# Lower parts of the first branch's, the gates' and the output projection's weights made by GpSimd, their products queued last

## The chip, the cores and the metric

The kernel runs on one core of a Trainium2 chip. The metric is the time of one execution on the device in microseconds (us), the median of several executions. An engine works through its own queue in order and waits at an instruction until the semaphores that it names have been raised: TensorE multiplies (PE in the profile, its weight loads PEld), VectorE (DVE) and ScalarE (ACT) do elementwise work, GpSimd (POOL) can do elementwise work too and cannot read PSUM, the memory that TensorE writes its sums to. SyncE (SP) issues DMAs.

## The reference

One layer of a diffusion backbone, for 512 latent tokens and 256 context tokens of 1024 channels, in 32-bit floats:

```python
h = rms_norm(x, g_norm1) * (1.0 + sc1) + sh1
aq, ak, av, dq, dk, dv, dz, da, db, ga, gd = split_cols(h @ w_in)
...
y_attn = window_ctx_attention(q_a, k_a, v_a, k_ac, v_ac, attn_sink)
o_dl, _, _ = bidir_delta(*dn_inputs(dq, dk, dv, da, db), s_cf, s_cb)
...
y_d = (rms_norm(o_d, dn_norm_g) * jax.nn.silu(heads(z, DN_HEADS))).reshape(z.shape)
y = jax.nn.sigmoid(gate_a) * (y_a @ w_br_attn) + jax.nn.sigmoid(gate_d) * (y_d @ w_br_dn)
...
x_new = x.astype(jnp.float32) + gt1 * merge(y_attn, o_dl, dz, ga, gd)
x_new = x_new + gt2 * mlp(x_new, sh2, sc2)
```

`bidir_delta` is a recurrence over chunks of 64 tokens in both directions, first over the context and then over the latent tokens. The MLP has 4096 hidden channels.

## The kernel before

**Products in three passes.** TensorE multiplies in a reduced 32-bit format (fp32r). To keep the accuracy, each operand is split into an upper part, the value rounded to that format, and a lower part, the rest. A product is the sum of three: upper weight by upper activation, upper weight by lower activation, lower weight by upper activation. A tile of 128 output channels with 1024 inputs has 8 blocks k and so 24 matmuls of 128x128 by 128x512; one with 512 inputs (a branch projection) has 4 blocks and 12 matmuls.

**Weights.** `wload` fetches a tile through SyncE's queue into one of four staging slots (`wr`), has ScalarE write the upper part (line 259) and then makes the lower part in one of three ways: line 266 subtracts on VectorE (raw minus upper); for the 14 attention and recurrence tiles (`late`), ScalarE writes the negated upper part and a DMA from GpSimd's queue adds the raw weights to it (lines 263 and 264). Upper and lower parts of the list `wq` have two slots each, `wh` and `wl`; the MLP's weights have buffers of their own (`m`). `wnext` hands out a tile and starts the load of the one after it, so that one tile is loaded ahead.

**The list.** After the 14 `late` tiles come 44 with line 266: three gate tiles of the second branch (kind GD), 8 tiles of the first branch's projection (`wbr[0]`, 4 blocks each), 17 gate tiles (8 GA, 4 DZ, 5 GD, 8 blocks each), 8 tiles of the second branch's projection (`wbr[1]`, 4 blocks) and 8 of the output projection (`wout`, 8 blocks).

**Who consumes them.** `gate_tiles` (line 1028) and `br_a` (line 1073) are generators that yield after each matmul: the recurrence's code runs some of their matmuls between its own steps (`run_fill`, `run_both`), as cover for the recurrence's waits. A step of the recurrence (`chain_step`) has for each direction: TensorE's products with the state (line 1152), VectorE's lines 1156 and 1157, TensorE's line 1164, VectorE's line 1170, TensorE's lines 1185 and 1189, VectorE's line 1201, which makes the next state. VectorE also makes later modulation vectors (`late_mod`, line 1094), spread over the same time. The second branch and the output projection use `mm3` (lines 317 to 319), which runs the three passes block by block. The second branch's result goes through lines 1348 and 1350 (VectorE) and a split (line 184 on ScalarE, line 185 on VectorE) into `Y`, the output projection's input. The last three output tiles are multiplied in column halves of 256, with `mm3` too, so that the next norm can begin on the first half; they hold three weight tiles, where `wh` and `wl` have two slots each.

**Order.** The program is written in one order, and a planner in the framework puts each engine's instructions in the order in which it expects them to become ready, by its own durations; the queues are fixed when the kernel is built. GpSimd's queue has, beside the 14 DMAs, memsets of 32x512 between the recurrence's matrices (lines 900, 901, 1288, 1289).

Of the kernel before, what the change touches and what calls it, by code (L numbers as in the profile page):

```python
# [12 lines left out]
ALU = mybir.AluOpType  # L13
# [21 lines left out]
ND1 = 3  # L35
# [3 lines left out]
KT = D // P  # L39
# [60 lines left out]
def tile_layer(ctx: ExitStack, tc: tile.TileContext, I: dict, out: bass.AP, dbg=None):  # L100
    nc = tc.nc
    V, A, G, PE = nc.vector, nc.scalar, nc.gpsimd, nc.tensor
# [30 lines left out]
    r32 = lambda ap: ap.bitcast(F32R)  # L133
# [116 lines left out]
        nc.sync.dma_start(out=raw, in_=src)  # L250
        return raw

    def wload(src, n=KT, bufs=None, raw=None, late=False):
        raw = wfetch(src, n) if raw is None else raw
        if bufs:
            hi, lo = (b.ap.rearrange("p (k c) -> p k c", k=KT) for b in bufs)
        else:
            hi, lo = (sb.tile([P, KT, P], F32, tag=t, bufs=NWS, name=nm(t))[:, :n] for t in ("wh", "wl"))
        h = A.activation(r32(hi), raw, AF.Copy)  # L259
        if not early:  # L260
            tc.add_manual_dep(h.ins, row_[0].ins.name, nosync, reason="behind the first row")
        if late:
            A.activation(r32(lo), hi, AF.Copy, scale=-1.0)
            G.dma_start(out=r32(lo), in_=src, accum_op=ALU.add)
        else:
            V.tensor_tensor(r32(lo), raw, hi, op=ALU.subtract)  # L266
        return r32(hi), r32(lo)

    early, EARLY = [], {T_DK: 0, T_DK + 1: 0, T_DK + 2: 0, T_DK + 3: 1}
# [39 lines left out]
            hs.pop(0)[0].free()  # L309


    def mm3(acc, w, xs, start=True, stop=True, ks=None):
        ks = list(range(len(xs))) if ks is None else ks
        n = len(ks)
        for i, k in enumerate(ks):
            xhi, xlo = xs[i]
            PE.matmul(acc, w[0][:, k, :], xhi, start=(start and i == 0), stop=False)  # L317
            PE.matmul(acc, w[0][:, k, :], xlo, start=False, stop=False)  # L318
            PE.matmul(acc, w[1][:, k, :], xhi, start=False, stop=(stop and i == n - 1))  # L319

    def modulate(t, src, r, sc, sh, hi, lo, eng=V):
        V.scalar_tensor_tensor(t, src, sc, r, op0=ALU.mult, op1=ALU.mult)
# [5 lines left out]
    hx, hc = [], []  # L328
# [11 lines left out]
    for kt in range(KT):  # L340
        t = alloc(512)
# [31 lines left out]
    for b in [wab_, xs_, cs_, rstd, scb]:  # L373
# [3 lines left out]
    gates = [(T_GD, i) for i in range(ND1)] + [(T_GA, i) for i in range(8)] + [(T_DZ, i) for i in range(4)]  # L377
    gates += [(T_GD, i) for i in range(ND1, 8)]
    wq = [(I["win"][t], KT, None, None, True) for t in (T_AK, *range(T_AQ, T_AQ + 3), T_AV, T_AQ + 3, *range(T_DV, T_DV + 4),
                                                        *range(T_DQ, T_DQ + 4))]  # L380
    wq += [(I["win"][t + i], KT) for t, i in gates[:ND1]]
    wq += [(I["wbr"][0, ct], 4) for ct in range(8)] + [(I["win"][t + i], KT) for t, i in gates[ND1:]]
    wq += [(I["wbr"][1, ct], 4) for ct in range(8)] + [(I["wout"][ct], KT) for ct in range(8)]
    wq = [lambda a=a: wload(*a) for a in wq]
    wn = [wq.pop(0)()]

# [298 lines left out]
    t, t2 = alloc(TOK), alloc(TOK)  # L685
# [18 lines left out]
    for q, (w, acc) in enumerate(early):  # L704
        conv(kT[q][:, :SEQ], acc.ap, 4 + q)
        acc.free()
        acc = bank()
# [310 lines left out]
    gat = []  # L1018
    szt, gdt = [], []

    def gate_tiles(todo):

        for kind, i in todo:
            w = wnext()
            acc = bank()
            for k in range(KT):
                for p, (x, y) in enumerate(((0, 0), (0, 1), (1, 0))):
                    PE.matmul(acc.ap, w[x][:, k, :], hx[k][y], start=(k == p == 0), stop=(k == KT - 1 and p == 2))  # L1028
                    yield
            if kind == T_GA:  # L1030
                g = alloc(SEQ)
                act(g.ap, acc.ap, AF.Tanh, scale=0.5)
                V.scalar_tensor_tensor(gat[i].ap, g.ap, 1.0, gat[i].ap, op0=ALU.add, op1=ALU.mult)
                g.free()
            else:
                t = alloc(SEQ, True)
                if kind == T_GD:
                    act(t.ap, acc.ap, AF.Tanh, scale=0.5)
                else:
                    silu2(t.ap, acc.ap)  # L1040
                (gdt if kind == T_GD else szt).append(t)
            acc.free()
# [22 lines left out]
    def br_a():  # L1065

        for ct in range(8):
            gat.append(alloc(SEQ, True))
            w = wnext()
            pa = bank()  # L1070
            for j in range(4):
                for p, (x, y) in enumerate(((0, 0), (0, 1), (1, 0))):
                    PE.matmul(pa.ap, w[x][:, j, :], r32(Q[y][:, :, j, :]), start=(j == p == 0), stop=(j == 3 and p == 2))  # L1073
                    yield
            A.activation(gat[ct].ap, pa.ap, AF.Copy)
            pa.free()
        for b in Qb:
            b.free()
# [263 lines left out]
    for ct in range(8):  # L1342
        w = wnext()
        run_late(ct % 2)
        pd = bank()
        mm3(pd.ap, w, [(r32(b[:, :512]), r32(b[:, 512:])) for b in yd])
        g = gdt[ct].ap
        V.scalar_tensor_tensor(g, g, 1.0, pd.ap, op0=ALU.add, op1=ALU.mult)
        pd.free()
        V.tensor_tensor(g, g, gat[ct].ap, op=ALU.add)  # L1350
        split(g, Y[ct][:, :512], Y[ct][:, 512:])
# [25 lines left out]
    for ct in range(8 - NHALF):  # L1377
        w = wnext()
        acc = bank()
        mm3(acc.ap, w, ys)  # L1380
        run_late(2)
        residual(ct, acc, slice(0, 512))
        acc.free()
# [203 lines left out]
```

## Time and profile before

| | |
|---|---|
| median of 3 executions | 911.67 us (911.41 to 916.42) |
| the profiled execution | 911.22 us, its span 909.5 us |
| PE busy | 97% of the span |
| DVE busy | 64% |
| ACT busy | 50% |
| POOL busy | 25.2 us, 40 instructions |

The span runs from the first instruction's start to the last one's end; 911.22 - 909.5 = 1.7 us lie around it. The page of the profile shows how long each engine was busy. A matmul's row lasts until its modelled end, and the next one starts before that, so PE's rows overlap and its busy share does not tell how dense its work is: start times do. In a list of waits, "A <- B: total, times, longest" says that A's engine stood idle ahead of A until B had ended. A timeline row gives start and length in us, engine, line, operation and tiles, and the idle time before it in brackets. A window row gives the stretch, its length, the busy time of each engine and the count of its instructions, the clock, and the DMA share.

By time, the first 295 us hold the norms, the input projections, attention and the preparation of the recurrence; from 295 to 376 and a little on, the context steps and the matrices of the latent steps, with the first branch's projection and gate tiles in between; to 470 the latent steps with gate tiles; from about 486 to 509 the second branch's projection, to 554 the output projection, and then the MLP to the end.

### The profile page before, as it was taken

What the parts mean: (1) busy time and instruction counts of PE and PEld (TensorE: products, weight loads), DVE (VectorE), ACT (ScalarE), POOL (GpSimd) and SP (SyncE); (2) the same over time, 40 slices, a digit from 0 to 9 for tenths busy, and PEclk for the clock granted to TensorE, in tenths of its full rate; (3) what the DMA queues carried; (4) which work ended last, traced back from release to release, by engine and by line L of the source; (5) the groups of instructions that cost most, each with busy time, mean ns of one, the idle gap of its engine ahead of it and who ended that gap; (6) DMA issues with size and microseconds to landing.
All of it is one profiled execution on the core that took longest, in us unless ns stands there. A gap on an engine that the chain in (4) does not pass through costs nothing.

```text
span 909.5 us, 16844 instructions
## 1 busy us (share of the span) xinstructions
PE 879.4 (97%) x7082; PEld 704.7 (77%) x7082; DVE 585.4 (64%) x999; ACT 454.9 (50%) x819; POOL 25.2 (3%) x40
## 2 busy tenths in 40 slices
PE   8999999999899999999999999999999999999998
PEld 5668777867677787777678789888888888888886
DVE  3578799887778997677867988941654335324511
ACT  6588755476568786465663445630452134113400
POOL 0010001010000002010000000000000000000000
PEclk9999999999999999999999999999999999999999
DMA  8671455533001133633316773640553224322111
GB/s 355 262 230 21 92 117 120 112 71 58 13 13 35 56 110 94 207 98 95 117 37 219 245 245 135 227 144 1 188 157 95 70 73 150 103 69 79 38 47 46
DMA packets 30460, 105.59 MB, mean 116 GB/s; under 512 B 3760, under 2 KB 4400, under 8 KB 29360
## 3 DMA queue, kind: packets, MB, share of 16 engines
q1 hardware_dynamic: 28368, 97.18, 33.1%
q0 software_dynamic: 2016, 7.34, 5.0%
q8 instruction: 55, 0.90, 0.4%
q14 instruction: 21, 0.17, 0.1%
HBM read 102.41 MB, written 2.10 MB: 115 GB/s over the span
## 4 chain that ended last, share of the span: by engine, by line
PE 80%; DVE 10%; ACT 5%; issue 2%; DMA 1%; SPq 0%; DVEq 0%; ACTq 0%
PE banks L319 16%; PE banks L317 16%; PE banks L318 16%; PE banks L1028 9%; PE banks L424 5%; PE banks L1073 2%; PE banks L429 2%; PE banks L586 2%; PE banks L596 1%; PE banks L1164 1%; ACT m L148 1%; PE banks L662 1%; PE banks L1185 1%; PE banks L1152 1%; PE banks L210 1%
## 5 line engine op out<-in xcount | busy, mean ns | idle before, releaser
L317 PE MATMUL banks<-m,m 128*128 128x512 f32 (+1 forms) x600 | 223.6, 377 | 2.6 <-DVE m L643 1.6
L318 PE MATMUL banks<-m,m 128*128 128x512 f32 (+1 forms) x600 | 224.5, 376 | 0.1
L319 PE MATMUL banks<-m,m 128*128 128x512 f32 (+1 forms) x600 | 224.2, 376 | 0.0
L259 ACT ACTIVATE m<-wr 128x1024 fp32r<-128x1024 f32 x68 | 71.8, 1059 | 155.1 <-PE banks L318 74.0
L317 PEld LDWEIGHTS banks<-m,m 128*128 128x128 f32 x600 | 111.8, 188 | 26.0 <-ACT m L323 2.8
L318 PEld LDWEIGHTS banks<-m,m 128*128 128x128 f32 x600 | 112.5, 188 | 21.9 <-DVE m L324 1.5
L319 PEld LDWEIGHTS banks<-m,m 128*128 128x128 f32 x600 | 112.4, 188 | 21.3 <-issue 1.2
L266 DVE TENSOR_TENSOR m<-wr,m 128x1024 fp32r<-128x1024 f32 x68 | 82.8, 1224 | 62.8 <-ACT m L259 31.2
L1028 PE MATMUL banks<-m,wh 128*128 128x512 f32 x320 | 104.5, 405 | 1.5 <-issue 0.8
L1471 DVE SCALAR_TENSOR_TENSOR m<-banks,modT,m 128x512 f32<-128x512 f32 x32 | 24.0, 750 | 105.3 <-PE banks L319 105.3
L259 ACT ACTIVATE wh<-wr 128x1024 fp32r<-128x1024 f32 (+1 forms) x58 | 54.6, 941 | 50.6 <-issue 11.4
L424 PE MATMUL banks<-m,wh 128*128 128x512 f32 (+1 forms) x320 | 75.9, 374 | 1.2 <-DVE m L823 1.2
L1028 PEld LDWEIGHTS banks<-m,wh 128*128 128x128 f32 x320 | 58.0, 188 | 14.2 <-issue 1.0
L1028 PE MATMUL banks<-m,wl 128*128 128x512 f32 x160 | 64.7, 405 | 0.0
L424 PEld LDWEIGHTS banks<-m,wh 128*128 128x128 f32 x320 | 53.0, 189 | 11.5 <-issue 1.9
L266 DVE TENSOR_TENSOR wl<-wr,wh 128x1024 fp32r<-128x1024 f32 (+1 forms) x44 | 45.2, 1028 | 16.6 <-ACT wh L259 16.5
L184 ACT ACTIVATE m<-m 128x512 fp32r<-128x512 f32 (+1 forms) x56 | 34.8, 629 | 38.1 <-DVE m L1454 21.5
L185 DVE TENSOR_TENSOR m<-m,m 128x512 fp32r<-128x512 f32 (+1 forms) x56 | 38.3, 689 | 21.6 <-ACT m L184 21.3
L1094 DVE SCALAR_TENSOR_TENSOR m<-wa,m 128x1024 f32<-128x1024 f32 x32 | 39.0, 1223 | 12.6 <-DMA wa<-in_wada 7.4
L317 PE MATMUL banks<-m,wh 128*128 128x512 f32 (+1 forms) x120 | 42.0, 352 | 0.0
L319 PE MATMUL banks<-m,wl 128*128 128x512 f32 (+1 forms) x120 | 42.0, 351 | 0.0
L318 PE MATMUL banks<-m,wh 128*128 128x512 f32 (+1 forms) x120 | 41.8, 349 | 0.0
(241 smaller groups left out, 1371.8 us busy)
## 6 DMA issues: line engine op xcount, KB each, us to landing
wr<-in_wm SPq DMA_DIRECT2D x64, 512.0 KB, 3.7
wr<-in_win SPq DMA_DIRECT2D x38, 512.0 KB, 3.7
wa<-in_wada SPq DMA_DIRECT2D x32, 512.0 KB, 4.1
m<-in_wada SPq DMA_DIRECT2D x8, 1024.0 KB, 12.3
wl<-in_win POOLq DMA_DIRECT2D x14, 512.0 KB, 5.7
m<-in_xT SPq DMA_DIRECT2D x8, 512.0 KB, 5.6
wr<-in_wbr SPq DMA_DIRECT2D x16, 256.0 KB, 2.6
wr<-in_wout SPq DMA_DIRECT2D x8, 512.0 KB, 4.6
```

Of the source, the lines that this page charges most:

```text
L184: A.activation(r32(hi), src, AF.Copy)
L185: (eng or V).tensor_tensor(r32(lo), src, hi, op=ALU.subtract)
L259: h = A.activation(r32(hi), raw, AF.Copy)
L266: V.tensor_tensor(r32(lo), raw, hi, op=ALU.subtract)
L317: PE.matmul(acc, w[0][:, k, :], xhi, start=(start and i == 0), stop=False)
L318: PE.matmul(acc, w[0][:, k, :], xlo, start=False, stop=False)
L319: PE.matmul(acc, w[1][:, k, :], xhi, start=False, stop=(stop and i == n - 1))
L424: PE.matmul(a, w[0][:, k, :], x, start=(k == 0 and x is xs[k][0]), stop=False)
L429: PE.matmul(a, w[1][:, k, :], xs[k][0], start=False, stop=(k == KT - 1))
L1028: PE.matmul(acc.ap, w[x][:, k, :], hx[k][y], start=(k == p == 0), stop=(k == KT - 1 and p == 2))
L1094: V.scalar_tensor_tensor(t.ap, wa, 0.5, scr.ap, op0=ALU.mult, op1=ALU.mult, accum_out=modT[:, grp, j:j + 1])
L1471: V.scalar_tensor_tensor(xn_[ct], acc.ap, modT[:, 3, ct:ct + 1], xn_[ct], op0=ALU.mult, op1=ALU.add)
```

## The change

Three things are edited.

1. `wload` gets an argument `eng`, by default VectorE, and the 41 tiles of the list from the first branch's projection on (all but the `late` ones and the first three gate tiles) have their lower part subtracted by GpSimd.
2. The order of a tile's matmuls in `gate_tiles` and `br_a`: first all products with the upper part of the weights (two for each block), then those with the lower part. The count of matmuls is the same, and so is that of yields.
3. `mm3` gets an argument `after` that does the same, and it is set for the second branch's projection and the first five tiles of the output projection. The last three, in halves, keep the old order.

```diff
-    def wload(src, n=KT, bufs=None, raw=None, late=False):
+    def wload(src, n=KT, bufs=None, raw=None, late=False, eng=V):
...
-            V.tensor_tensor(r32(lo), raw, hi, op=ALU.subtract)
+            eng.tensor_tensor(r32(lo), raw, hi, op=ALU.subtract)
...
-    def mm3(acc, w, xs, start=True, stop=True, ks=None):
+    def mm3(acc, w, xs, start=True, stop=True, ks=None, after=False):
...
-            PE.matmul(acc, w[1][:, k, :], xhi, start=False, stop=(stop and i == n - 1))
+            if not after:
+                PE.matmul(acc, w[1][:, k, :], xhi, start=False, stop=(stop and i == n - 1))
+        for i, k in enumerate(ks if after else ()):
+            PE.matmul(acc, w[1][:, k, :], xs[i][0], start=False, stop=(stop and i == n - 1))
...
-    wq += [(I["wbr"][0, ct], 4) for ct in range(8)] + [(I["win"][t + i], KT) for t, i in gates[ND1:]]
-    wq += [(I["wbr"][1, ct], 4) for ct in range(8)] + [(I["wout"][ct], KT) for ct in range(8)]
+    wg = [(I["wbr"][0, ct], 4) for ct in range(8)] + [(I["win"][t + i], KT) for t, i in gates[ND1:]]
+    wg += [(I["wbr"][1, ct], 4) for ct in range(8)] + [(I["wout"][ct], KT) for ct in range(8)]
+    wq += [(*a, None, None, False, G) for a in wg]
...
+    def lo_last(n):
+        return [(0, y, k) for k in range(n) for y in range(2)] + [(1, 0, k) for k in range(n)]
...
-            for k in range(KT):
-                for p, (x, y) in enumerate(((0, 0), (0, 1), (1, 0))):
-                    PE.matmul(acc.ap, w[x][:, k, :], hx[k][y], start=(k == p == 0), stop=(k == KT - 1 and p == 2))
-                    yield
+            for p, (x, y, k) in enumerate(lo_last(KT)):
+                PE.matmul(acc.ap, w[x][:, k, :], hx[k][y], start=(p == 0), stop=(p == 3 * KT - 1))
+                yield
...
-        mm3(pd.ap, w, [(r32(b[:, :512]), r32(b[:, 512:])) for b in yd])
+        mm3(pd.ap, w, [(r32(b[:, :512]), r32(b[:, 512:])) for b in yd], after=True)
...
-        mm3(acc.ap, w, ys)
+        mm3(acc.ap, w, ys, after=True)
```

`br_a` is edited as `gate_tiles` is, with 4 blocks in place of 8.

More of the change, by code (lines that the diff above doesn't have):

```diff
@@ L1070, in br_a @@
             pa = bank()
[L1071 to L1074, printed above, removed]
+            for i, (x, y, j) in enumerate(lo_last(4)):
+                PE.matmul(pa.ap, w[x][:, j, :], r32(Q[y][:, :, j, :]), start=(i == 0), stop=(i == 11))
+                yield
             A.activation(gat[ct].ap, pa.ap, AF.Copy)
```

## The prediction

> **What bounds the kernel now.** I read the page's head first (which engine is full), then the busy time by stage, then the waits in the stages that the change touches, then single instructions at those waits.
>
> ```profile
> span 909.5 us, 16844 instructions
> ...
> PE 879.4 (97%) x7082; PEld 704.7 (77%) x7082; DVE 585.4 (64%) x999; ACT 454.9 (50%) x819; POOL 25.2 (3%) x40
> ...
> core 0: us, PE busy (x) PEld busy (x) DVE busy (x) ACT busy (x) POOL busy (x), PEclk, DMA share, GB/s
> 562.00:909.50 347.50, 343.43 (x1558) 285.56 (x1556) 149.97 (x184) 102.61 (x134) 0.00 (x0) 1.00 0.32 100
> 486.00:509.00 23.00, 23.00 (x100) 18.28 (x99) 20.86 (x35) 10.85 (x17) 0.00 (x0) 1.00 0.75 247
> 509.00:554.00 45.00, 44.98 (x262) 39.36 (x261) 36.84 (x57) 17.09 (x24) 0.00 (x0) 1.00 0.73 236
> 295.00:400.00 105.00, 102.86 (x1514) 79.94 (x1510) 83.71 (x147) 72.16 (x153) 9.21 (x16) 1.00 0.38 119
> 400.00:470.00 70.00, 65.71 (x1328) 50.82 (x1329) 50.89 (x118) 42.69 (x143) 0.00 (x0) 1.00 0.28 85
> ```
>
> The matrix engine PE is busy 879.4 of 909.5 us, at a granted clock of 1.00 in every row. From 562 us to the end the two MLP products run 1558 matmuls in 347.5 us with PE busy 343.43, and nothing that the change edits is in there. Before the first branch's first weights all instructions stay what they are. So the question is the stretch between. In 295 to 400 PE idles 105 - 102.86 = 2.1 us, in 400 to 470 4.3 us, from 486 to 554 nothing. These 6.4 us are about all that an engine off PE can hand back there: 0.7% of the run, less than the 1% that a measurement of this kernel can tell from no change. PE's own work in the stretch (the same matmuls and weight loads, in another order) stays.
>
> A row of PE is 0.39 us long where the next starts 0.23 us later, so the real pace has to come from start times:
>
> ```profile
> 504.76 0.40 PE L317 MATMUL banks<-m,wh 128*128 128x512 f32 x1
> ...
> 505.68 0.40 PE L318 MATMUL banks<-m,wh 128*128 128x512 f32 x1
> 505.98 0.50 PE L319 MATMUL banks<-m,wl 128*128 128x512 f32 x1
> 506.32 0.39 PE L317 MATMUL banks<-m,wh 128*128 128x512 f32 x1
> ```
>
> The five starts from 504.76 to 505.68 are 0.23 us apart (0.92 / 4). A tile of 12 matmuls (a branch projection) takes 2.8 us at that pace, one of 24 (a gate or output tile) 5.6 us. At 505.98 the lower-part matmul (line 319, operand wl) starts 0.07 us late, and the next 0.34 later: it waited for its weights.
>
> ```profile
> DVE wl L266 <- ACT wh L259: 16.5, 15, 3.5
> ...
> PEld banks L1164 <- DVE m L1157: 4.0, 6, 1.2
> ...
> PEld banks L319 <- DVE wl L266: 0.8, 4, 0.3
> ```
>
> Lateness of lower parts costs PE's weight loads 0.8 us in four places, all in the dense stage. The large wait is that of the chain step's product (line 1164) for VectorE's line 1157: 4.0 us in six places, as its weight loads show it. VectorE (DVE) itself stood 16.5 us behind ScalarE's upper parts. So the lower parts hurt mainly by standing in VectorE's queue ahead of the chain.
>
> **The change part by part.** *Moved off VectorE.*
>
> ```profile
> L266 DVE TENSOR_TENSOR wl<-wr,wh 128x1024 fp32r<-128x1024 f32 x28 | 34.2, 1223 | 16.2 <-ACT wh L259 16.1
> ...
> L266 DVE TENSOR_TENSOR wl<-wr,wh 128x512 fp32r<-128x512 f32 x16 | 11.0, 686 | 0.4 <-ACT wh L259 0.4
> ...
> L901 POOL MEMSET m<- 32x512 f32 x6 | 3.1, 522 | 134.2 <-PE banks L1185 125.8 <-PE banks L586 8.3
> ...
> L1288 POOL MEMSET m<- 32x512 f32 x4 | 3.0, 744 | 23.5 <-DVE m L1285 23.5
> ```
>
> Of the 28 subtracts of 128x1024 three (the first gate tiles) stay; 25 x 1.223 and 16 x 0.686 = 41.6 us leave VectorE. What PE gets of it is to be read where a chain waits:
>
> ```profile
> 394.34 1.23 DVE L266 TENSOR_TENSOR wl<-wr,wh 128x1024 fp32r<-128x1024 f32 x1 [2.44 <-ACT wh L259]
> 395.48 1.28 DVE L1278 TENSOR_TENSOR m<-m,banks 128x512 f32<-128x512 f32 x2
> ...
> 399.92 0.75 DVE L1157 SCALAR_TENSOR_TENSOR m<-m,m 128x256 f32<-128x256 f32 x2
> ...
> 393.32 1.10 PE L777 MATMUL banks<-m,m 64*32 64x64 f32 x64
> ...
> 400.48 1.15 PE L1164 MATMUL banks<-m,m 64*64 64x64 f32 x32 [1.74 <-DVE m L1157]
> ...
> 434.26 1.22 DVE L266 TENSOR_TENSOR wl<-wr,wh 128x1024 fp32r<-128x1024 f32 x1
> 435.39 0.42 DVE L1157 SCALAR_TENSOR_TENSOR m<-m,m 128x256 f32<-128x256 f32 x1
> ...
> 435.87 0.68 PE L1164 MATMUL banks<-m,m 64*64 64x64 f32 x16 [1.09 <-DVE m L1157]
> ```
>
> At 394.34 the subtract (1.23 us) stands ahead of line 1278 (395.48), whose product (line 777) ended at 393.32 + 1.10 = 394.42; VectorE is then busy without a gap to line 1157, for which PE waits 1.74 us at 400.48. Without it, line 1278 starts 1.0 us sooner: -1.0. At 434.26 the subtract stands directly ahead of line 1157 (435.39), and PE waits 1.09 us: -1.1. Of the 0.8 us of late lower parts, 0.6 goes (the rest is the last tile, below). Together -2.7 us. The 16.5 us of VectorE's own waiting goes too, but no other wait of PE in these rows ends on it, so I give it nothing more.
>
> *The price on GpSimd.* No row shows GpSimd (POOL) with two inputs. The nearest is its memset of 512 elements per partition, 0.52 us, so 1.0 us for 1024: the low end, with nothing read. Two inputs and one output, each at that pace, give 3.1 us, and 4.3 with one VectorE instruction of 1.22 us ahead of it: the high end. I take 2.1 us for 1024 and 1.05 for 512, the memset's pace twice, since the row is nearest in kind (one pass of the port each way). The 41 subtracts are then 69 us on an engine that was busy 25.2. [...]
>
> *Cover for the slower subtract.* The lower matmuls now come after 16 (or 8) upper ones: 16 x 0.23 = 3.7 us (or 1.8) more time, against 2.1 - 1.22 = 0.9 us (or 0.4) more work. Before, no gate or branch matmul waits for a lower part ahead of the dense stage. So 0, at the high price too (3.1 us more against 3.7). The weight staging buffer (four slots) is held 0.9 us longer and its next DMA issue on SyncE's queue waits as long; the upper part's slot comes free 8 matmuls, 1.9 us, sooner, so ScalarE waits less. PE waits for neither: 0. On GpSimd's queue the subtracts meet the memsets of lines 900, 901, 1288 and 1289; a memset behind a subtract comes up to 2.1 us late, which would show in the chain's next product, and a subtract behind a memset that waits has a tile of time and more. I take 0; the high end is one such delay, 2.1.
>
> *The last output tiles* are the place without cover: they run in column halves with the old order (the lower part third), and two slots serve three tiles.
>
> ```profile
> 546.20 1.22 DVE L266 TENSOR_TENSOR wl<-wr,wh 128x1024 fp32r<-128x1024 f32 x1
> ...
> 547.24 0.28 PE L318 MATMUL banks<-m,wh 128*128 128x256 f32 x1
> 547.48 0.38 PE L319 MATMUL banks<-m,wl 128*128 128x256 f32 x1
> ```
>
> The eighth tile's lower part ends at 547.42 and PE's lower matmul starts at 547.48, 0.24 after its predecessor where 0.12 is the pace of half tiles: just in time. On GpSimd it ends 0.9 us later: +0.9 (from 0, if other matmuls are queued between, to 3.1 at the high price).
>
> *The shared way into SBUF.* Where the two engines meet in this trace:
>
> ```profile
> 386.03 0.74 POOL L1288 MEMSET m<- 32x512 f32 x1 [12.86 <-DVE m L1285]
> ...
> 385.55 1.83 DVE L1285 COPY m<-m 32x512 f32<-32x512 f32 x4
> ```
>
> Four copies of line 1285 take 1.83 us on VectorE, and the memsets of line 1288 that lie among them take 744 ns on average, where those of line 901, of the same shape, take 522. The two engines hold each other up by some 0.2 us. If a subtract that reads on GpSimd holds up VectorE's two-input instructions for its whole length, line 1157 is one of them (m<-m,m in its row). In 400 to 470:
>
> ```profile
> L266 DVE TENSOR_TENSOR wl<-wr,wh 128x1024 fp32r<-128x1024 f32 x6 | 7.3, 1223 | 5.0 <-ACT wh L259 5.0
> L1157 DVE SCALAR_TENSOR_TENSOR m<-m,m 128x256 f32<-128x256 f32 x16 | 6.5, 421 | 0.2
> ```
>
> Six subtracts and eight pairs of line 1157 (0.81 us a pair): a pair meets a subtract with 6 x (2.1 + 0.8) / 70 = 0.25, so two pairs do, held 1.05 us on average; the queued gate matmuls cover about half: +1.0 (ends 0 and 6.6, below).
>
> *The order.* Instruction order on each queue comes from the framework's planner, with its own durations: the source has the gate tiles after all transposes, the trace has not.
>
> ```profile
> 473.34 0.48 PE L1028 MATMUL banks<-m,wh 128*128 128x512 f32 x1
> 473.66 1.06 PE L1323 MATMUL banks<-c_ident,m 128*128 128x128 f32 x8
> ```
>
> A GpSimd subtract in its plan shifts what is queued next to what, in the whole stretch. I take 0; the ends are the 3.7 us of PE's idle that are left after -2.7, either way.
>
> Sum: -2.7 + 0.9 + 1.0 = -0.8 us on the profiled execution's 911.22 gives 910.4. The median of the three runs is 911.67, 0.45 above that execution, which would make it 910.9. I put 910.6.
>
> **The rivals.** *The port binds the chain (916.0).* Every subtract in 400 to 470 holds up a pair for its full 2.1 us, of which the queued matmuls hide 1.0: 6 x 1.1 = 6.6 in place of 1.0, so 911.2 - 2.7 + 0.9 + 6.6 = 916.0. For it: the 744 against 522 ns. Against: VectorE's chain instructions mostly take one input from PSUM (lines 1156, 1170), and the subtract starts after ScalarE's upper part, at the tile's border, where few pairs stand. [...]
>
> *GpSimd cannot keep the pace of the second branch (slower, 924).* From 486 to 509 a tile lasts 2.8 us.
>
> ```profile
> L1350 DVE TENSOR_TENSOR m<-m,m 128x512 f32<-128x512 f32 x7 | 4.8, 685 | 0.0
> L1348 DVE SCALAR_TENSOR_TENSOR m<-m,banks 128x512 f32<-128x512 f32 x7 | 4.8, 682 | 0.9 <-PE banks L319 0.9
> L185 DVE TENSOR_TENSOR m<-m,m 128x512 fp32r<-128x512 f32 x6 | 4.1, 690 | 1.1 <-ACT m L184 1.0
> L1094 DVE SCALAR_TENSOR_TENSOR m<-wa,m 128x1024 f32<-128x1024 f32 x3 | 3.7, 1223 | 4.4 <-PE banks L1028 4.4
> ```
>
> Per tile VectorE has 0.69 + 0.69 us of two-input work and half an instruction of 1.22 (2.0 us), and the subtract comes on top if they exclude each other. Before, VectorE did 2.0 + 0.68 + 0.69 = 3.35 us per tile and ended 8 x 0.57 = 4.6 us late without idling PE. The loss is then 8 x (2.0 + x - 2.8) - 4.6 for a subtract of x us: below zero at 1.05, over 9.1 us (1%) from x = 2.5 on, and 13 us at x = 3.0: 924. Against: 2.5 us would be almost five times the memset.
>
> *All waits go (906).* VectorE's queue is free early, ScalarE's too, and the new plan fills the rest: most of the 6.4 us, 5, is gained: 906.2. For it: all those waits name VectorE or "issue". Against: line 1157 also waits behind other work than the subtract (at 399.92 it is the end of a row of VectorE work from 395.48 on).
>
> *It does nothing (911.2):* the subtracts on VectorE were hidden but at two places, and a new plan could put other work there.
>
> **How the numbers follow.** Forecast, -3 to +2 us: 0.48, with the case of nothing in it. Port binds: 0.18. All waits go: 0.20. Pace lost: 0.08. A replanned order outside these ends: 0.06, half of it to each side. The range of 8 in 10 goes from 905.0, a little below the case of all waits gone, to 918.0, above the port's case with one further wait like that at 400.48; the pace case is left out. Faster by over 1% (below 902.5) would need more than the stretch's idle: 0.03, the replanned order alone. Slower by over 1%: the pace case and the other half of the replanned order, 0.11. Within 1%: 0.86.
>
> **What would show it.** Right: subtracts of 1.9 to 2.4 us on POOL; the waits at 400.48 and 435.87 shorter; line 319 no longer waiting for line 266 but in the last output tile; PE's busy time from 486 to 554 equal. The port: line 1157 or 1094 longer than 0.42 and 1.22 us, or starting late while a subtract runs, and more of line 1164's waits. The pace: idle on PE in 486 to 509 ended by POOL. Wrong altogether: a difference before the first branch or after 562 us, or PE idle of several us that names POOL's memsets.

## The result, and the profile after

The changed kernel takes 937.67 us (median of 4 executions, 933.1 to 941.84), the kernel before in the same session 912.27 us (911.41 to 916.42). The ratio is 1.0268, with a 95% interval of 1.021 to 1.0326: the change costs 25 us. The forecast was 910.6 us with a range of 905 to 918, so it was wrong, and by far more than the range allowed.

From line 856 on, the changed kernel's lines stand four to six lower in the file: line 1028 is now 1034, 1033 is 1039, 1073 is 1078, 1094 is 1099, 1156 is 1161, 1157 is 1162, 1164 is 1169, 1170 is 1175, 1189 is 1194, 856 and 857 (the inversion of the chunk matrices) are 860 and 861, 1278 is 1283, 1350 is 1355. `mm3`'s lower parts are line 320 in the old order and 322 in the new. The profiled execution took 936.8 us. The page's head:

```profile
span 935.0 us, 16860 instructions
...
PE 890.6 (95%) x7082; PEld 712.6 (76%) x7082; DVE 591.6 (63%) x958; ACT 455.3 (49%) x819; POOL 111.5 (12%) x81
```

Two things differ from before. PE's busy time has grown by 890.6 - 879.4 = 11.2 us with the same 7082 matmuls, and its idle time from 909.5 - 879.4 = 30.1 to 935.0 - 890.6 = 44.4 us, by 14.3. VectorE lost 41 subtracts, and still it is busy 591.6 us instead of 585.4. Without these subtracts its rows of the kernel before cover 549.2 us (neighbouring rows overlap a little, so this is more than 585.4 less their 41.6). So its other instructions take some 42 us longer. The view of instruction groups by shape shows which (busy time, mean ns of one, idle time ahead), first the kernel before for three groups that were not shown yet:

```profile
L1156 DVE TENSOR_TENSOR m<-banks,eg 128x256 f32<-128x256 f32 x22 | 9.0, 418 | 0.3 <-PE banks L1152 0.3
...
L1033 DVE SCALAR_TENSOR_TENSOR m<-m,m 128x512 f32<-128x512 f32 x8 | 5.5, 686 | 1.4 <-ACT m L148 1.4
...
L856 DVE TENSOR_TENSOR m<-m 128x300 f32<-128x300 f32 x2 | 0.9, 470 | 0.1
```

and after, VectorE and GpSimd:

```profile
L1099 DVE SCALAR_TENSOR_TENSOR m<-wa,m 128x1024 f32<-128x1024 f32 x32 | 42.2, 1324 | 15.2 <-DMA wa<-in_wada 10.0 <-PE banks L1034 4.8
...
L1039 DVE SCALAR_TENSOR_TENSOR m<-m,m 128x512 f32<-128x512 f32 x8 | 14.8, 1853 | 10.9 <-ACT m L148 10.9
...
L1162 DVE SCALAR_TENSOR_TENSOR m<-m,m 128x256 f32<-128x256 f32 x22 | 12.4, 578 | 0.4
...
L1355 DVE TENSOR_TENSOR m<-m,m 128x512 f32<-128x512 f32 x8 | 9.7, 1213 | 0.1
...
L1161 DVE TENSOR_TENSOR m<-banks,eg 128x256 f32<-128x256 f32 x22 | 8.9, 418 | 1.9 <-PE banks L1157 1.8
```

```profile
L266 POOL TENSOR_TENSOR wl<-wr,wh 128x1024 fp32r<-128x1024 f32 x25 | 62.3, 2493 | 126.7 <-PE banks L1034 48.6 <-ACT wh L259 35.4 <-PE banks L322 21.6
L266 POOL TENSOR_TENSOR wl<-wr,wh 128x512 fp32r<-128x512 f32 x16 | 24.2, 1511 | 115.7 <-PE banks L1034 74.0 <-ACT wh L259 30.9 <-PE banks L1157 4.1
```

The groups that grew most read two tiles from SBUF: line 1162 went from 421 to 578 ns on average, line 1355 from 685 to 1213, line 1039 from 686 to 1853, line 1099 from 1223 to 1324. GpSimd's subtracts themselves take 2.49 and 1.51 us on average. Line 1161, which stands directly ahead of line 1162 and takes one of its inputs from PSUM (`banks`), stayed at 418 ns to the digit. One group with a single SBUF input grew too: the copies of line 1285 before, 1290 after, from 488 to 763 ns. One of the eight makes the difference, with 2.60 us beside the subtract that starts at 397.72; the others are as they were.

Where PE waits, in the list of waits from 263 us to the end of the output projection, before and after (total, times, longest):

```profile
PE banks L1164 <- DVE m L1157: 3.9, 4, 1.7
```

```profile
PE banks L1169 <- DVE m L1162: 9.3, 5, 3.1
...
PE banks L318 <- DVE m L185: 4.6, 2, 3.7
...
PE banks L1190 <- DVE m L1175: 3.7, 1, 3.7
...
PE banks L320 <- POOL wl L266: 1.2, 1, 1.2
```

The wait for line 1157 was 3.9 us in four places and is 9.3 in five; three waits are new, 4.6, 3.7 and 1.2 us. Only the last names GpSimd. Over their whole length the two lists add up to 7.6 and 21.9 us, which differ by the 14.3 us of new idle time. Three stretches of the timeline show how the others come about. A step of the recurrence (start, length, engine):

```profile
455.46 0.75 DVE L1161 TENSOR_TENSOR m<-banks,eg 128x256 f32<-128x256 f32 x2
...
455.71 2.35 POOL L266 TENSOR_TENSOR wl<-wr,wh 128x1024 fp32r<-128x1024 f32 x1 [8.61 <-ACT m L1181]
456.12 2.55 DVE L1162 SCALAR_TENSOR_TENSOR m<-m,m 128x256 f32<-128x256 f32 x2
...
458.39 0.88 PE L1169 MATMUL banks<-m,m 64*64 64x64 f32 x18 [2.35 <-DVE m L1162]
```

With no subtract beside it the pair of line 1162 takes 0.75 us (at 411.28). Here it starts while GpSimd subtracts, and takes 2.55; it ends 0.6 us after the subtract does, about one instruction and a half. The pair of line 1161 ran beside the same subtract for 0.5 us unhurt. PE stood 2.35 us for it. In the context steps:

```profile
336.94 2.34 POOL L266 TENSOR_TENSOR wl<-wr,wh 128x1024 fp32r<-128x1024 f32 x1 [1.92 <-ACT wh L259]
337.12 2.49 DVE L860 TENSOR_TENSOR m<-m 128x300 f32<-128x300 f32 x1
339.54 0.41 DVE L1175 TENSOR_TENSOR m<-banks,eg 128x256 f32<-128x256 f32 x1
...
340.00 1.22 PE L1190 MATMUL banks<-m,m 64*64 64x64 f32 x18 [3.74 <-DVE m L1175]
```

Line 860 has two SBUF inputs (both of tile `m`) and took 0.47 us before at this shape; here 2.49, until 0.3 us after the subtract's end. Line 1175, for which PE waits 3.74 us, is not held up itself. It stands behind line 860 in VectorE's queue. And at the border from the second branch to the output projection:

```profile
523.36 5.85 POOL L266 TENSOR_TENSOR wl<-wr,wh 128x1024 fp32r<-128x1024 f32 x2 [2.24 <-PE banks L322]
...
523.58 3.44 DVE L1099 SCALAR_TENSOR_TENSOR m<-wa,m 128x1024 f32<-128x1024 f32 x1
...
527.55 2.22 DVE L185 TENSOR_TENSOR m<-m,m 128x512 fp32r<-128x512 f32 x1
...
529.82 0.50 PE L318 MATMUL banks<-m,wh 128*128 128x512 f32 x1 [3.66 <-DVE m L185]
```

Two subtracts of 1024, for the first output tiles, run while VectorE still works off the branch. The modulation vector takes 3.44 instead of 1.22 us, the split of line 185 takes 2.22 instead of 0.69, and the first output tile's twelfth matmul waits 3.66 us for that split.

The other half of the loss, PE's longer busy time, goes with the granted clock, 0.984 over the span and 1.000 before. The view of stretches (length, busy time and count of PE, PEld, DVE, ACT and POOL, then the granted clock):

```profile
243.90:247.20 3.30, 2.99 (x10) 2.61 (x11) 1.09 (x4) 1.02 (x3) 0.00 (x0) 0.50 0.01 2
335.00:339.00 4.00, 1.26 (x6) 0.71 (x4) 3.86 (x5) 2.33 (x4) 2.08 (x2) 1.00 0.41 161
339.50:346.00 6.50, 6.00 (x46) 5.31 (x47) 6.22 (x18) 2.20 (x7) 0.00 (x0) 0.50 0.26 82
411.00:417.50 6.50, 5.75 (x100) 4.74 (x100) 2.49 (x8) 2.16 (x8) 0.05 (x1) 0.50 0.00 0
500.86:524.00 23.14, 23.13 (x100) 18.48 (x99) 19.09 (x25) 9.66 (x15) 11.66 (x8) 1.00 0.71 238
530.60:537.00 6.40, 4.98 (x10) 3.18 (x11) 6.29 (x11) 1.06 (x2) 0.00 (x0) 0.50 0.79 269
537.40:544.00 6.60, 6.60 (x29) 5.34 (x29) 4.16 (x8) 2.40 (x3) 2.81 (x2) 1.00 0.62 209
```

Before, no row showed a clock below 1.00. After, it is 0.50 in five stretches, each beginning near the end of a pause of PE or just behind one: from 243.8 us for 3.41 us, from 339.4 for 6.83, from 411.1 for 6.83, from 458.9 for 3.41, from 530.5 for 6.83, together 27.3 us. The pauses ahead of them are 2.10, 3.74, 3.10, 2.35 and 3.66 us. At half clock PE ran 10 matmuls in 4.98 us of busy time (530.6 to 537), behind it 29 in 6.60; their starts are 0.43 us apart from 535.05 to 536.33, and 0.23 from 539.13 to 540.51. If all of it went at half pace, half of 27.3 us, 13.7, would be lost, as an estimate from these rows; measured were 11.2.

So 14.3 us of new idle time and 11.2 of slower matmuls make the 25.5 us between the two spans. The same product's start or end in both traces tells where they arose:

| | before, us | after, us | later by |
|---|---|---|---|
| first gate matmul starts | 263.18 | 265.11 | 1.9 |
| last matmul of the first branch ends | 331.80 | 336.26 | 4.5 |
| last half product (line 777) ends | 394.42 | 404.80 | 10.4 |
| last product of the recurrence (line 1189) ends | 466.44 | 481.23 | 14.8 |
| second branch's projection starts | 485.93 | 500.86 | 14.9 |
| last product of the output projection ends | 554.55 | 580.15 | 25.6 |
| end of the span | 909.5 | 935.0 | 25.5 |

The 1.9 us of the first row are not the change's doing: its first subtract on GpSimd starts at 287.24 us, and the half clock from 243.8 follows a pause that the kernel before has too (the last section comes back to it). The second branch itself kept its pace (100 matmuls in 23.1 us, as before); the 10.7 us of the sixth row came behind it, with the wait at 529.82, the half clock from 530.5, and the last tiles.

### The profile page after: what moved, and what is told of

The parts are those of the page before. It is cut to its first block, busy times and chain, and to the rows that moved or that the text cites. A ratio compares the mean times of both kernels' runs of the same rounds, so it can differ in the third digit from the quotient of the medians.

```text
span 935.0 us, 16860 instructions
## 1 busy us (share of the span) xinstructions
PE 890.6 (95%) x7082; PEld 712.6 (76%) x7082; DVE 591.6 (63%) x958; ACT 455.3 (49%) x819; POOL 111.5 (12%) x81
## 4 chain that ended last, share of the span: by engine, by line
PE 74%; DVE 16%; ACT 4%; issue 2%; DMA 2%; SPq 0%; POOLq 0%; DVEq 0%; ACTq 0%
PE banks L317 15%; PE banks L318 15%; PE banks L320 14%; PE banks L1034 11%; PE banks L428 5%; PE banks L433 2%; PE banks L590 2%; DVE m L860 2%; DVE m L861 1%; PE banks L600 1%; DVE m L185 1%; DVE m L1099 1%; PE banks L1169 1%; PE banks L1190 1%; DVE m L1355 1%
## 5 line engine op out<-in xcount | busy, mean ns | idle before, releaser
L266 POOL TENSOR_TENSOR wl<-wr,wh 128x1024 fp32r<-128x1024 f32 (+1 forms) x41 | 86.5, 2110 | 242.4 <-PE banks L1034 122.7
L1034 PE MATMUL banks<-m,wh 128*128 128x512 f32 x320 | 89.5, 418 | 0.0
L428 PE MATMUL banks<-m,wh 128*128 128x512 f32 (+1 forms) x320 | 75.9, 375 | 1.2 <-DVE m L827 1.2
L1034 PEld LDWEIGHTS banks<-m,wh 128*128 128x128 f32 x320 | 60.1, 196 | 13.7
L428 PEld LDWEIGHTS banks<-m,wh 128*128 128x128 f32 x320 | 53.0, 189 | 11.5 <-issue 1.9
L185 DVE TENSOR_TENSOR m<-m,m 128x512 fp32r<-128x512 f32 (+1 forms) x56 | 41.3, 743 | 21.6 <-ACT m L184 21.2
L1099 DVE SCALAR_TENSOR_TENSOR m<-wa,m 128x1024 f32<-128x1024 f32 x32 | 42.2, 1324 | 15.2 <-DMA wa<-in_wada 10.0
L318 PE MATMUL banks<-m,wh 128*128 128x512 f32 (+1 forms) x120 | 43.3, 361 | 4.6 <-DVE m L185 4.6
L317 PE MATMUL banks<-m,wh 128*128 128x512 f32 (+1 forms) x120 | 43.7, 364 | 1.0 <-ACT m L184 0.8
L1034 PE MATMUL banks<-m,wl 128*128 128x512 f32 x160 | 44.0, 403 | 0.0
L433 PE MATMUL banks<-m,wl 128*128 128x512 f32 (+1 forms) x160 | 38.3, 369 | 0.0
```

What stands on the lines that cost most here:

```text
L185: (eng or V).tensor_tensor(r32(lo), src, hi, op=ALU.subtract)
L266: eng.tensor_tensor(r32(lo), raw, hi, op=ALU.subtract)
L428: PE.matmul(a, w[0][:, k, :], x, start=(k == 0 and x is xs[k][0]), stop=False)
L433: PE.matmul(a, w[1][:, k, :], xs[k][0], start=False, stop=(k == KT - 1))
L1034: PE.matmul(acc.ap, w[x][:, k, :], hx[k][y], start=(p == 0), stop=(p == 3 * KT - 1))
L1099: V.scalar_tensor_tensor(t.ap, wa, 0.5, scr.ap, op0=ALU.mult, op1=ALU.mult, accum_out=modT[:, grp, j:j + 1])
```

## The experiments

Two theories stood against each other. **A:** an instruction of GpSimd that reads SBUF holds up VectorE's instructions with two inputs in SBUF, and so the chains that PE waits for. **B:** the planner lays the queues out differently once lower parts come from GpSimd and upper products come first, and the recurrence's cover falls in the wrong places. A second question was what a pause of PE costs beyond its own length. Unless said otherwise the edit is to the changed kernel, and the ratio is to the kernel before on the same chip, with its 95% interval. The extra instructions of the reader, writer and copy runs write to a buffer whose value is no longer needed.

**Order alone, GpSimd alone.** The first run leaves the lower parts on VectorE and keeps the new order; the second leaves them on GpSimd and takes the order back.

```diff
-    wq += [(*a, None, None, False, G) for a in wg]
+    wq += [(*a, None, None, False, V) for a in wg]
```

> The new order of the matmuls with all lower parts on VectorE, as before. Theory A (GpSimd's subtract holds up VectorE's two-input instructions, as line 1162 took 2.21 us in place of 0.42 in the changed kernel's trace): the loss is gone, 909 to 914 us, and no instruction of line 1162 above 0.45 us. Theory B (the new order, or the order that the planner makes of it, costs the time): 930 to 938 us. No PE gap above 2.5 us after 263 us by A.

```diff
-        return [(0, y, k) for k in range(n) for y in range(2)] + [(1, 0, k) for k in range(n)]
+        return [(x, y, k) for k in range(n) for x, y in ((0, 0), (0, 1), (1, 0))]
...
-        mm3(pd.ap, w, [(r32(b[:, :512]), r32(b[:, 512:])) for b in yd], after=True)
+        mm3(pd.ap, w, [(r32(b[:, :512]), r32(b[:, 512:])) for b in yd])
...
-        mm3(acc.ap, w, ys, after=True)
+        mm3(acc.ap, w, ys)
```

> The subtracts on GpSimd with the old order of the matmuls (lower part third). Theory A: as slow as the whole change, 930 to 942 us, a little slower if lower parts now also come late (0.9 us a tile at most, in the dense stage). Theory B: 909 to 914 us.

Order alone: 912.72 us, ratio 0.9994 (0.9977 to 1.0011). GpSimd alone: 938.08 us, 1.0272 (1.0245 to 1.0298). The new order does nothing that can be measured, and the engine that subtracts makes the whole difference. B falls as far as it concerns the order of the products. What the planner does with GpSimd's subtracts in its plan is not told apart from A by these two runs.

**One stage at a time.** GpSimd for the first 25 tiles (first branch and gates), then for the last 16 (second branch and output) alone.

```diff
-    wq += [(*a, None, None, False, G) for a in wg]
+    wq += [(*a, None, None, False, G if n < 25 else V) for n, a in enumerate(wg)]
```

> GpSimd subtracts for the first branch's projection and the 17 gate tiles, VectorE for the second branch's and the output projection. The changed kernel is 14.9 us behind at the start of the second branch (500.86 against 485.93 us) and 25.6 at the end of the output tiles. By theory A the time is 912 + 15 = 927, give or take 3; if one stage's delay frees another's waits, less. If the second stage alone is to blame: 912.

```diff
-    wq += [(*a, None, None, False, G) for a in wg]
+    wq += [(*a, None, None, False, V if n < 25 else G) for n, a in enumerate(wg)]
```

> The other half: VectorE for the first branch and the gate tiles, GpSimd for the second branch's and the output projection. By theory A 912 + 10.7 = 923, give or take 3 (PE waits 4.1, 1.1, 1.4 and 0.8 us for line 185 or ScalarE behind it, and 1.4 us in the last output tile). If the loss comes from the recurrence alone: 912.

First stage: 925.08 us, 1.0128 (1.0102 to 1.0154), so 11.7 us. Last stage: 919.13 us, 1.0072 (1.0046 to 1.0098), 5.8 us, less than expected. Both stages lose, and neither is the whole. The sum is 17.5 of some 25 us; part of the rest is clock, since in the profiled executions the first-stage kernel stood at half clock for 13.6 us (granted clock 0.992 over the span) and the last-stage kernel for 6.8 (0.996), the whole change for 27.3 (0.984). Like pauses brought different drops: in the whole change 2.35 us at 456.04 were followed by 3.41 us of half clock, 2.30 us at 314.88 by none. The last section has what the traces show of that.

**Reader or writer.** With the lower parts on VectorE, GpSimd gets extra work for each of the 41 tiles: a subtract with two inputs (reader), two memsets of the tile (writer), or one copy (one input). All three write the same staging slot, so all three hold it; the writer does so twice.

```diff
-    wq += [(*a, None, None, False, G) for a in wg]
+    wq += [(*a, None, None, False, A) for a in wg]
...
-            eng.tensor_tensor(r32(lo), raw, hi, op=ALU.subtract)
+            V.tensor_tensor(r32(lo), raw, hi, op=ALU.subtract)
+        if eng is A:
+            G.tensor_tensor(raw, hi, ones.unsqueeze(1).broadcast_to([P, n, P]), op=ALU.subtract)
```

> The order-only kernel, all lower parts on VectorE, plus one more GpSimd instruction for each of the 41 tiles, whose result nobody reads: a subtract of two inputs in SBUF (the upper part and a constant) over the staging buffer. Theory A (a GpSimd instruction that reads two inputs excludes VectorE's two-input ones): as slow as the whole change or slower, since VectorE has its own 41.6 us as well: 925 to 945 us, with line 1162 up to 2.4 us. If the loss had to do with the lower parts coming from GpSimd (late weights, its queue), the time is that of order only.

```diff
+        if eng is A:
+            for _ in range(2):
+                G.memset(raw, 0.0)
```

> The same with two memsets of the staging buffer in place of the extra subtract: about 2.0 us for 1024 elements by the memset row (0.52 us for 512), so GpSimd is about as long busy, but reads nothing. Theory A in its narrow form (only reads exclude VectorE's second input): the time of order only within 2 us, line 1162 at 0.42. If any GpSimd instruction excludes VectorE: as the extra reader.

```diff
+        if eng is A:
+            G.tensor_copy(raw, hi)
```

> The order-only kernel plus one GpSimd copy with one input (the upper part over the staging buffer) for each of the 41 tiles, whose result nobody reads. If any read of GpSimd excludes VectorE's second input, two-input lines are held for the copy's length, about 1 to 1.5 us by the memset's 0.955 for 1024: 920 to 930 us. If only two-input instructions of GpSimd do: the time of order only, 910 to 914.

The groups of GpSimd's extra work and of two of VectorE's lines with two SBUF inputs (the modulation vectors, and line 1033 of the kernel before), reader first:

```profile
L268 POOL TENSOR_TENSOR wr<-wh,ones 128x1024 f32<-128x1024 f32 x25 | 65.3, 2614 | 134.4 <-DVE wl L266 101.3 <-issue 24.4 <-DMA wa<-in_wada 7.7
...
L1101 DVE SCALAR_TENSOR_TENSOR m<-wa,m 128x1024 f32<-128x1024 f32 x32 | 47.0, 1472 | 14.4 <-DMA wa<-in_wada 14.2
...
L1041 DVE SCALAR_TENSOR_TENSOR m<-m,m 128x512 f32<-128x512 f32 x8 | 7.5, 938 | 0.3 <-ACT m L148 0.3
```

```profile
L269 POOL MEMSET wr<- 128x1024 f32 x50 | 47.7, 955 | 128.0 <-DVE wl L266 80.4 <-issue 16.2 <-ACT m L1184 12.5
...
L1102 DVE SCALAR_TENSOR_TENSOR m<-wa,m 128x1024 f32<-128x1024 f32 x32 | 38.9, 1223 | 9.4 <-DMA wa<-in_wada 9.0
...
L1042 DVE SCALAR_TENSOR_TENSOR m<-m,m 128x512 f32<-128x512 f32 x8 | 5.5, 682 | 0.9 <-ACT m L148 0.9
```

```profile
L268 POOL COPY wr<-wh 128x1024 f32<-128x1024 f32 x25 | 33.0, 1322 | 142.9 <-DVE wl L266 103.8 <-issue 24.8 <-ACT m L1183 13.4
...
L1101 DVE SCALAR_TENSOR_TENSOR m<-wa,m 128x1024 f32<-128x1024 f32 x32 | 41.5, 1298 | 11.5 <-DMA wa<-in_wada 11.3
...
L1041 DVE SCALAR_TENSOR_TENSOR m<-m,m 128x512 f32<-128x512 f32 x8 | 6.3, 791 | 0.2 <-ACT m L148 0.2
```

With the reader line 1033's group takes 938 ns on average, with the copy 791, with the writer 682, as undisturbed (686); and the modulation vectors 1472, 1298 and 1223 ns. The times:

| | GpSimd busy, us | VectorE busy, us | longer than its own work by | time, us | ratio (95%) |
|---|---|---|---|---|---|
| order alone | 25.2 | 585.3 | 0 | 912.72 | 0.9994 (0.9977 to 1.0011) |
| writer | 89.5 | 585.8 | 0.5 | 911.28 | 0.9974 (0.9961 to 0.9988) |
| copy | 74.9 | 595.2 | 9.9 | 914.31 | 0.9999 (0.9986 to 1.0012) |
| reader | 117.0 | 622.7 | 37.4 | 943.51 | 1.0322 (1.029 to 1.0354) |
| the change | 111.5 | 591.6 | 42.7 | 937.67 | 1.0268 (1.021 to 1.0326) |

The fourth column compares VectorE's busy time with that of order alone; for the change, with the 548.8 us that order alone's rows cover without the 41 subtracts. In the writer run GpSimd was busy 64 us more, at a ratio of 0.9974, so more GpSimd work in the plan does not by itself cost time. A stands, for these runs. The reader's 2.4 us for line 1162 did not come: the longest of its instructions took 0.84 us, and other lines had the long holds. The reader's time is not quite the price of the holds alone, since a subtract keeps its staging slot longer than two memsets do (2.61 against 1.91 us for a tile of 1024), and the modulation weights are fetched into the same four slots.

By its time alone, the copy run would have spoken for the second branch of its expectation; the rows show that the copies held VectorE up too, 791 ns against 682. So here being held up was not yet time: 9.9 us of VectorE are lost to it and none of the run, with copies of 1.06 to 1.32 us. That the queued matmuls cover holds so short is the likely reason; it was not tried by itself.

**Short holds.** The change itself, with GpSimd's subtract cut into one instruction for each block of 128 columns (264 in place of 41), to leave VectorE room in between.

```diff
-            eng.tensor_tensor(r32(lo), raw, hi, op=ALU.subtract)
+            for k in range(n) if eng is G else (slice(None),):
+                eng.tensor_tensor(r32(lo)[:, k], raw[:, k], hi[:, k], op=ALU.subtract)
```

> The changed kernel with each GpSimd subtract cut into pieces of 128 columns (8 or 4 instructions a tile). Theory A says that a VectorE instruction waits until the running GpSimd instruction ends: then no wait is longer than one piece (2.37 / 8 = 0.3 us, and somewhat more for the start of each instruction), a two-input line of 0.42 us shows at most about 0.8, and PE's waits of 2.3 to 3.7 us go: 914 to 922 us. If the block lasts over all that GpSimd has queued, or VectorE loses by the sum of GpSimd's time alone: 930 to 940.

```profile
L267 POOL TENSOR_TENSOR wl<-wr,wh 128x128 fp32r<-128x128 f32 x264 | 148.5, 597 | 177.6 <-PE banks L1035 76.0 <-ACT wh L259 50.8 <-issue 28.7
...
L1040 DVE SCALAR_TENSOR_TENSOR m<-m,m 128x512 f32<-128x512 f32 x8 | 6.5, 814 | 13.5 <-ACT m L148 13.5
...
L1163 DVE SCALAR_TENSOR_TENSOR m<-m,m 128x256 f32<-128x256 f32 x22 | 10.0, 469 | 0.4
```

923.83 us, 1.0103 (1.008 to 1.0126), just above the expected stretch. GpSimd is busy longer (173.3 us) and VectorE is held up less: 564.9 us busy, 16.1 us over its own work instead of 42.7. Line 1163, the 1157 of before, averages 469 ns instead of 578, and line 1040, the 1033 of before, 814 instead of 1853. The loss goes from 25 to 10 us. Here the length of a single GpSimd instruction (597 ns on average in place of 2493 and 1511) counted for more than GpSimd's total.

**What a pause of PE costs.** The kernel before, with one pause made by hand ahead of the last eight MLP tiles: their first input is copied onto itself once, or five times, by ScalarE after the last activation is ready. The values stay.

```diff
         xs = [(r32(b[:, :512]), r32(b[:, 512:])) for b in act_]
+        if hf == 3:
+            zc = small([P, 1], "zc", bufs=1)
+            V.tensor_scalar(zc, act_[-1][:, 0:1], 0.0, None, op0=ALU.mult)
+            for _ in range(1):
+                A.activation(xs[0][0], act_[0][:, :512], AF.Identity, bias=zc)
```

> The kernel before with one pause of TensorE built in, ahead of the last eight MLP tiles: their first operand is copied onto itself once on ScalarE behind the last activation (values unchanged). PE then waits about 2 us. Expected: 912 + 2 = 914 us, granted clock 1.00 throughout.

> The same with five copies, each 0.63 us by the split's row: PE waits about 4.6 us. If a pause costs its own length only: 2.5 us over the kernel with one copy, 917. If TensorE's clock drops to half behind a pause of more than 3 us and stays there for 3.4 to 6.8 us, as in the five stretches of the changed kernel: 1.7 to 3.4 us on top, 918 to 920, and a stretch of clock 0.5 behind the pause.

Stretches behind the pause, with one copy and with five:

```profile
865.30:868.90 3.60, 0.04 (x1) 0.00 (x0) 1.45 (x3) 1.94 (x3) 0.00 (x0) 1.00 0.00 0
869.30:872.70 3.40, 3.40 (x10) 2.63 (x9) 0.00 (x0) 0.00 (x0) 0.00 (x0) 0.51 0.00 0
873.00:876.40 3.40, 3.40 (x17) 2.81 (x16) 0.08 (x1) 0.00 (x0) 0.00 (x0) 1.00 0.00 0
```

```profile
870.60:876.30 5.70, 5.70 (x13) 4.45 (x14) 0.00 (x0) 0.00 (x0) 0.00 (x0) 0.50 0.00 0
```

The first expectation missed: one copy made a pause of 3.62 us, and a half clock followed. Behind the pause PE runs 10 matmuls in 3.4 us at half clock, and 17 in the next 3.4. The time is 919.27 us, 1.0055 (1.0035 to 1.0074), which is 3.2 to 6.8 us more than before: 3.62 of pause and 1.7 lost in a stretch of 3.41 at half clock make 5.3. Five copies make a pause of 6.63 us; the half clock begins within it, at 866.1, and lasts 5.7 us beyond its end, 2.9 us lost. That makes 9.5 us; measured were 921.81 us, 1.0081 (1.0054 to 1.0108), which is 4.9 to 9.9 us more than before. The second expectation missed too, on the slow side of its 918 to 920, as the pause was 2 us longer than taken. In both runs the loss agrees with the pause's length and half of the stretch at half clock that was left behind it, 5.3 and 9.5 us by this estimate.

**VectorE freed without GpSimd.** Order alone, with the 17 gate tiles made like the `late` tiles: ScalarE writes the negated upper part, and a DMA adds the raw weights.

```diff
-    wq += [(*a, None, None, False, G) for a in wg]
+    wq += [(*a, None, None, 8 <= n < 25, V) for n, a in enumerate(wg)]
```

> The order-only kernel with the lower parts of the 17 gate tiles made without a subtract: ScalarE writes the negated upper part (1.06 us) and a DMA adds the raw weights to it, as the 14 earlier tiles do. Nothing of GpSimd then reads two inputs, and 17 x 1.22 = 21 us leave VectorE. If freeing VectorE in the recurrence is worth what the prediction gave it (waits of 1.0 and 1.1 us), 2 us faster than order only: 909 to 911 us. If ScalarE's extra 18 us come into the chain instead (lines 1181 and 1204 stand in its queue), 913 to 918.

PE's waits from 263 us on:

```profile
PE banks L882 <- issue: 3.2, 1, 3.2
...
PE banks L1169 <- DVE m L1162: 2.8, 3, 1.4
```

915.6 us, 1.003 (1.0007 to 1.0052). VectorE is relieved (566.6 us busy), and the wait for line 1157 falls from 3.9 to 2.8 us: the gain that the prediction hoped for exists, and is about 1 us. But elsewhere PE now stands 3.2 us, for a reason that the trace does not name ("issue"), and a half clock of 6.83 us follows (granted clock 0.994 over the span). Whether the DMAs or the new plan make that pause was not tried.

No kernel here beats the one before by anything useful. The writer run's 0.3% (about 2.4 us) comes with memsets that do nothing; its profiled execution had no stretch at half clock at all (granted clock 1.000).

## Why the prediction was wrong

**The price on GpSimd** was about right: 2.1 us taken for 1024, 2.34 to 2.49 measured for 20 of the 25; 1.05 for 512, 1.51 measured on average and 1.30 at 519.82 us, where it is nearly shortest. The 2.1 us were the memset's pace taken twice; no run shows the passes of a port that they were put down to.

**The gains at 400.48 and 435.87 (-1.0 and -1.1)** failed: the first turned into a loss, of the second a third came (PE waits 0.74 us at 447.43 in place of 1.09). The first place shows why:

```profile
404.01 2.36 POOL L266 TENSOR_TENSOR wl<-wr,wh 128x1024 fp32r<-128x1024 f32 x1 [3.10 <-PE banks L1034]
404.44 2.48 DVE L1039 SCALAR_TENSOR_TENSOR m<-m,m 128x512 f32<-128x512 f32 x1 [0.72 <-ACT m L148]
...
406.84 1.27 DVE L1283 TENSOR_TENSOR m<-m,banks 128x512 f32<-128x512 f32 x2
...
411.75 0.48 PE L1169 MATMUL banks<-m,m 64*64 64x64 f32 x4 [3.10 <-DVE m L1162]
```

The subtract has left VectorE's queue, but VectorE's line 1039, of 0.69 us, is held up behind it for 2.48, and line 1283 starts at 406.84, 2.0 us after its product's end (404.81), where it was 1.1. PE's wait went from 1.74 to 3.10 us. The work moved to another engine and kept its place in VectorE's time.

**The cover for slower lower parts (0)** held: no product waits for a lower part but in the last output tiles. **The last output tile (+0.9)** was 1.22 us: the subtract ran from 570.31 to 572.67, and line 320 waited for it. The mechanism was right and the size nearly. **GpSimd's memsets (0)** cost PE nothing: no wait of PE after 263 us names them.

**The order (0)** held: 0.9994 for order alone.

**The port (+1.0, at most 6.6)** is the step that failed. No run shows a port as such; the runs show longer VectorE instructions beside a GpSimd that reads (line 1162's 578 ns in place of 421). The term asked how often line 1157 meets a subtract in 400 to 470, and nothing else. There its count came true: two of line 1162's instructions were held, at 445.69 (1.69 us in place of 0.42) and at 456.12 (2.21), so by 1.5 us on average where 1.05 was taken; the first cost PE nothing more, the second 2.35 us and a half clock behind it. In that stage, from the last half product to the end of the recurrence, 4.4 us were lost, clock included, within the bound. But 8.5 us had been lost between 263 and 405 and 10.7 were lost after 500, where the sum had no such term. Lines 856 and 857 stand in VectorE's queue ahead of the context steps, lines 1350, 185 and 1094 ahead of `Y`, and all read two SBUF tiles. The evidence was in the prediction's own rows: VectorE was busy 20.86 of 23.00 us in the second branch, which leaves 2.1 us; the change takes 8 x 0.69 = 5.5 us off it and lets GpSimd read for 8 x 1.3 = 10.4. VectorE's lag then met the first output tiles' subtracts at 523, and PE paid 3.66 us at 529.82.

The rival "the port binds the chain" therefore named what was measured, instructions of VectorE held beside a subtract, with a chance of 0.18 and a price from one stage of three. As it was put, it was wrong: not every subtract from 400 to 470 us met a pair of line 1157, and its argument against itself, that few pairs stand where a subtract starts, held. That its 6.6 us lie near the 4.4 is luck, since the 4.4 hold a wait of 3.10 us and a half clock that line 1039 made, which it left out. "GpSimd cannot keep the pace of the second branch" was wrong as put: the branch kept 23.1 us, and its subtracts took 1.29 to 2.28 us, 1.60 on average, below its point of 2.5.

**The clock** was missing altogether. The prediction quoted 1.00 in every row as a given of this kernel, and priced each wait at its own length. Four of the five drops follow pauses that the holds made. With 11.2 of 25.5 us it is nearly half of the loss, though some 1.7 of it, from the first drop, are not the change's doing. The stretches at half clock lasted 3.41 or 6.83 us, behind pauses of 2.10 to 3.74 us; the last section has what the traces show of it.

**The bound** at the start, 6.4 us of idle time from 295 to 554, was a bound on the gain alone. The prediction used what was left of it for both ends of the order's term, and looked for losses only where PE idled already. A PE without idle time says nothing of what it can lose.

## What to carry to other kernels

Before work is moved from VectorE to GpSimd, add up stage by stage what GpSimd will read and what VectorE does with two SBUF inputs, as if both stood in one queue; 41.6 us moved off VectorE came back to it as 42 us of longer instructions here. If the stage has no such room, shorter pieces did less harm than long ones here (25 us of loss became 10 with pieces of 128 columns), and instructions that only write did none here (0.5 us on VectorE, a ratio of 0.9974). Price a pause of TensorE at its length, and add 1.7 to 3.4 us of lost clock, an estimate: half of the 3.41 and 6.83 us that the stretches at half clock lasted in the changed kernel. From 263 us on its pauses of 3.10, 3.66 and 3.74 us were followed by one, and of those of 2.30 and 2.35 us the second alone; with the pauses of 3.62 and 6.63 us made by hand one came too.

## What the runs showed of the hardware that was not expected

The clock drop was not the same each time. Ahead of the recurrence PE pauses for 2.09 us from 241.61 us on in the kernel before, and for 2.10 from 242.11 on in the changed one. In the profiled execution of the first no half clock follows, in that of the second one of 3.41 us.

In the changed kernel the starts of the half clock lie 95.57, 71.68, 47.79 and 71.68 us apart, 28, 21, 14 and 21 times 3.413. With its trace cut into stretches of that length, with a border at each of these starts, the stretches directly ahead of a half clock are:

```profile
240.40:243.81 3.41, 1.71 (x12) 1.10 (x11) 3.35 (x7) 1.64 (x3) 0.00 (x0) 1.00 0.26 77
335.97:339.38 3.41, 0.29 (x2) 0.00 (x0) 3.31 (x4) 1.38 (x2) 2.34 (x1) 1.00 0.40 160
407.65:411.06 3.41, 1.00 (x5) 0.48 (x3) 3.31 (x8) 2.25 (x4) 1.42 (x2) 1.00 0.41 144
455.44:458.85 3.41, 1.06 (x18) 0.62 (x18) 3.41 (x6) 2.14 (x9) 2.35 (x1) 1.00 0.48 154
527.12:530.53 3.41, 0.50 (x1) 0.19 (x1) 3.41 (x4) 0.12 (x1) 2.10 (x1) 1.00 0.71 207
```

PE is busy in them for 0.29 to 1.71 us. In the other 200 of these stretches at full clock, from 200 us to PE's last product, it is busy for at least 1.73. That lowest one is:

```profile
315.49:318.90 3.41, 1.73 (x34) 1.50 (x35) 3.34 (x8) 0.02 (x1) 1.35 (x1) 1.00 0.50 156
```

The pause of 2.30 us from 314.88 on lies across its start, and no drop followed. This is what one trace shows; that it is a rule is not shown. In order alone PE's longest wait after 263 us is 1.7 us; in its trace a half clock follows a stretch in which PE is busy for 1.68 us:

```profile
398.30:401.71 3.41, 1.68 (x36) 1.20 (x34) 2.82 (x7) 2.39 (x6) 1.10 (x2) 1.00 0.00 1
401.72:405.12 3.40, 3.40 (x68) 2.53 (x68) 1.17 (x4) 1.05 (x4) 0.00 (x0) 0.50 0.02 5
```

The spread of the kernel before goes with the clock. Each execution has its mean granted clock on record: of its 52 executions in the sessions of the experiments, the nine at 1.000 took 910.35 to 911.90 us, the eleven at 0.996 took 913.47 to 915.92.

A copy on GpSimd with a single input held up two-input instructions of VectorE as well: line 1033's group averaged 791 ns beside it and 682 beside memsets. On VectorE's side a copy with a single SBUF input was held once, for 2.60 us in place of 0.41 (line 1290 at 397.84 in the changed kernel); one case is not a rule.
